# First attention layer of a four-layer network: both score maps in the array's rows, float32 values, rotation sums on VectorE

## The chip, the cores and the metric

The kernel runs on one core of one Trainium2 chip, in one launch. The metric is device time in microseconds (us). A core has TensorE (PE in the profile, with its weight loads as PEld), VectorE (DVE), ScalarE (ACT), GpSimd (POOL) and the queue that issues most DMAs (SP). Each engine works through its own instructions in the order in which they stand; semaphores tie the engines together. TensorE's results land in PSUM, from where DVE or ACT fetch them; POOL works on SBUF alone.

## The reference, cut to what matters

Two blocks of two layers each, 512 tokens, width 1024, all in float32. The change touches the attention of the first two layers:

```python
# layer 1: differential attention, 8 heads, two maps of 64 columns each, values of 128 columns
q = apply_rope(q, cos, sin) * 64 ** -0.5          # x1*cos - x2*sin, x1*sin + x2*cos
k = apply_rope(k, cos, sin)
for i in range(4):                                # blocks of 128 queries, keys up to the block's end
    sc = einsum('bqhmd,bkhmd->bhmqk', q[:, q0:kend], k[:, :kend])
    allowed = chunk(key) <= chunk(query)          # chunks of 64 tokens
    p = softmax(where(allowed, sc, neg))
    a = p[:, :, 0] - lam * p[:, :, 1]
    outs.append(einsum('bhqk,bkhe->bqhe', a, v[:, :kend]))
o = rms_norm(concat(outs), subln_g) * (1 - lambda_init)
x = layer_norm(alpha * x + o @ w_o);  x = layer_norm(alpha * x + swiglu(x))
# layer 2: attention over the own chunk and eight chunks before, 16 heads of 64, with a bias by distance
```

Then follow the second layer's feed-forward part and a second block of two layers (gated recurrences, a convolution and a feed-forward part), which the change leaves alone.

## The kernel before

Activations lie with features on the partitions and tokens along the row. A factor of a large product is held as two parts in the faster format fp32r: `hi`, a rounded copy that ACT writes (L150), and `lo`, the rest, which a subtraction on DVE writes (L151; POOL where `sub` is given). A product is three matmuls, hi·hi, hi·lo and lo·hi (`mm3`, L117 to L119; `dense`, L128 to L132). Plain float32 operands make one matmul in the code, which stands in the trace as two records.

**First layer (`attention_a`), about 25 to 306 us of the span.** For a head, `project` makes q, k (two maps each) and v from `xh`, `xl` and the weights `wA`, in four tiles of 128 tokens with 24 matmuls each. For each tile DVE forms four products with cos and sin out of PSUM (L379 to L382), POOL makes a difference and a sum of them (L383, L384), and v is split in hi and lo. `turn` transposes the rotated tiles and splits them (`qh`, `ql`, `kh`, `kl`). For a query block i of n = 128(i+1) keys, `scores` runs for each of the two maps a product of 64 rows, and a matmul of one row that adds the mask to the last 64 keys (L410); then DVE takes the maximum (L412) and ACT the exponential with its sum (L414). A map has a PSUM tile `sc` of its own, of which there are two. `mix` scales and subtracts the maps (L421 to L424), transposes the result (L427) and splits each of the 10 blocks of a head in `aTh` and `aTl`. `values` multiplies with v (`av`), forms the norm with matmuls of one column (L174), a chain of small DVE operations and matmuls against the identity (L202), and writes `oh`, `ol`.

`attend` takes head h block by block, and between blocks a tile of the projection of head h+1. Heads 0 to 5 go through all four blocks; heads 6 and 7 first through blocks 0 and 1, then 2 and 3, so that the first half of the output projection (`oh`, `ol` with `wo_a`, L128 to L132) has work for TensorE at the end. The framework's scheduler sorts all instructions by priority and its own estimate of time; `tc.high_priority` lets a group go ahead.

**Second layer (`attention_b`), about 720 to 942 us.** It already has the pattern that the change brings to the first: one tile `scs` of two banks for two heads, whose matmuls of 64 rows alternate (L541), a DVE instruction that adds the bias and takes the extreme in one pass (L546), the exponential in place (L548), transposes (L555), one copy for a whole block row from `tr` to `aT` on ACT (L558) and float32 value products (L566).

Of the kernel before, what the change touches and what calls it, by code (L numbers as in the profile page):

```python
# [18 lines left out]
P = 128  # L19
# [25 lines left out]
AT_OFF = (0, 512, 896, 1152, 1280)  # L45
HID1 = ((0, 5), (5, 10), (10, 14), (14, 22))
# [281 lines left out]
def attention_a(c):  # L328
    nc, tc, ap = c.nc, c.tc, c.ap
    with ExitStack() as st:  # L330
# [18 lines left out]
        nc.vector.tensor_scalar_sub(nlam[:, 1:2], nlam[:, 1:2], lambda_init(0))  # L349
        gsub = one.tile([P, 1], F32, name="gsub")  # L350
# [9 lines left out]
        def project(h):  # L360
            w = c.weight(ap["wA"][h], KT, 384, 2, then=load_x if h == 0 else None)
            v = [c.t(pool, [P, 4, P], F32R, t) for t in ("vh", "vl")]
            rots = c.t(pool, [P, 4, 4, 64], F32, "rot", 2)
            if h == 0:
                pss = [c.t(psum, [P, SEQ], F32, t, n) for t, n in (("sc", 2), ("sc", 2), ("av", 1))] + [c.bank()]
                c.dense_tk([ps[:, :384] for ps in pss], w, [(tt * P, tt * P + P) for tt in range(4)])
            for tt in range(4):
# [5 lines left out]
                qk = ps[:, :256].rearrange("p (g x) -> p g x", g=4)  # L373
                cs = cos[:, tt:tt + 1, :].to_broadcast([P, 4, 32])
                sn = sin[:, tt:tt + 1, :].to_broadcast([P, 4, 32])
                rot = rots[:, tt]
                tmp = c.t(pool, [P, 4, 64], F32, "rtmp")
                x1, x2 = qk[:, :, 0:32], qk[:, :, 32:64]
# [22 lines left out]
        def scores(h, i):  # L401
            qh, ql, kh, kl = made[h][0]
            n = (i + 1) * P
            qs = slice(i * P, i * P + P)
            ps_, sums = [], c.t(pool, [P, 2], F32, "sums")
            for m in range(2):
                ms = slice(m * 64, m * 64 + 64)
                sc = c.t(psum, [P, 512], F32, "sc", 2)
                c.mm3(sc[:, :n], qh[ms, qs], ql[ms, qs], kh[ms, :n], kl[ms, :n], True, False)
                nc.tensor.matmul(sc[:, n - 64:n], c.maskl, c.maskr, start=False, stop=True)  # L410
                mx = c.t(pool, [P, 1], F32, "mx")
                nc.vector.tensor_reduce(mx, sc[:, :n], AX.X, ALU.max, negate=True)  # L412
                p = c.t(pool, [P, SEQ], F32, f"p{m}", 3)
                nc.scalar.activation(p[:, :n], sc[:, :n], AF.Exp, bias=mx, scale=1.0, accum_out=sums[:, m:m + 1])  # L414
                ps_.append(p)
            return ps_, sums

        def mix(i, ps_, sums, aT):
# [9 lines left out]
            for j in range(i + 1):  # L428
                f = AT_OFF[j] + (i - j) * P
                c.split(*(t[:, f:f + P] for t in aT), tr[:, j * P:j * P + P])  # L430

        def values(h, aT, r0, r1):
# [3 lines left out]
            for j in range(r1):  # L436
                f = max(r0 - j, 0) * P
                t = slice(AT_OFF[j] + f, AT_OFF[j] + (r1 - j) * P)
                c.mm3(o[:, j * P + f:b], v[0][:, j, :], v[1][:, j, :], aT[0][:, t], aT[1][:, t], j == 0, j == r1 - 1)
# [12 lines left out]
        def attend(h, r0, r1, fill, last):  # L452
# [3 lines left out]
            aT = [c.t(pool, [P, 1280], F32R, t, 1) for t in ("aTh", "aTl")]  # L456
# [1043 lines left out]
```

## Time and profile before

| | us |
|---|---|
| median of 3 runs | 2801.31 |
| lowest, highest | 2797.56, 2808.92 |
| the profiled execution | 2814.44 |
| its span | 2812.4 |
| PE, PEld busy in the span | 2681.8 (95%), 2462.6 (88%) |
| DVE, ACT, POOL busy | 1955.0 (70%), 1228.4 (44%), 868.9 (31%) |

The profiled execution is 13 us longer than the median of the others. Ends of matmuls are modelled, so the time that a matmul takes up is read from its start to the start of the next one, not from its length. The granted clock (PEclk) is 1.00 at TensorE's full 2.4 GHz, 0.50 at 1.2 GHz. In a timeline, "x2" merges neighbours of one kind, and a bracket gives the idle time ahead of an instruction and who ended it.

### The profile page before, as it was taken

Reading aid. Unit: us, or ns where it says so; the run is one execution under the profiler, and the core shown is the slowest. Engines: PE = TensorE matmul, PEld = TensorE weight load, DVE = VectorE, ACT = ScalarE, POOL = GpSimd, SP = SyncE. Lnnn points to the kernel's source line nnn. Section 1 sums busy time; section 2 is a strip of 40 time slices with the busy share of each in tenths; the row PEclk is TensorE's granted clock in tenths of the full one; section 3 lists DMA queues with packets and bytes.
Section 4 is the critical chain, followed back from the end, with each engine's and each line's share of the span. In section 5 each row is a group of like instructions: output and inputs, shape, how many; then the busy total and the mean of one; then the engine's idle time right before and its main releaser. Section 6 shows DMA issues by size and latency. Waiting matters only on the chain. (4 is left out here: it accounts for less than half of the span.)

```text
span 2812.4 us, 49226 instructions
## 1 busy us (share of the span) xinstructions
PE 2681.8 (95%) x19432; PEld 2462.6 (88%) x19432; DVE 1955.0 (70%) x3974; ACT 1228.4 (44%) x2325; POOL 868.9 (31%) x711
## 2 busy tenths in 40 slices
PE   8999899999999999999999998999899999899997
PEld 7888899999777899899788898999898889889997
DVE  6775777676534777677766468888955645888895
ACT  4343444444544554444533335444533333445452
POOL 1110225572230225463012006545401200454550
PEclk9997999999999999999999999999999999999998
DMA  4111223323322222323211221322321211223222
GB/s 131 46 48 61 73 78 106 91 91 105 106 77 89 82 89 91 96 93 102 64 61 46 61 87 35 98 97 100 96 78 54 60 53 53 60 95 100 95 79 70
DMA packets 73799, 224.69 MB, mean 80 GB/s; under 512 B 9248, under 2 KB 11344, under 8 KB 73568
## 3 DMA queue, kind: packets, MB, share of 16 engines
q1 hardware_dynamic: 70736, 217.22, 24.8%
q8 instruction: 152, 2.49, 0.4%
q10 hardware_dynamic: 2304, 3.15, 0.3%
q0 software_dynamic: 528, 1.19, 0.1%
q14 instruction: 79, 0.65, 0.1%
HBM read 219.43 MB, written 2.10 MB: 79 GB/s over the span
## 5 line engine op out<-in xcount | busy, mean ns | idle before, releaser
L128 PE MATMUL mm<-xh,whi 128*128 128x256 f32 (+4 forms) x1976 | 583.9, 296 | 23.2 <-ACT tail L1254 11.3
L130 PE MATMUL mm<-xl,whi 128*128 128x256 f32 (+4 forms) x1976 | 580.4, 294 | 0.6 <-DVE xl L151 0.6
L132 PE MATMUL mm<-xh,wlo 128*128 128x256 f32 (+4 forms) x1976 | 578.6, 293 | 0.0
L151 DVE TENSOR_TENSOR wlo<-wraw,whi 128x1024 fp32r<-128x1024 f32 (+3 forms) x426 | 474.7, 1117 | 100.0 <-ACT whi L150 98.8
L150 ACT CAST whi<-wraw 128x1024 fp32r<-128x1024 f32 (+3 forms) x444 | 384.8, 883 | 326.3 <-PE mm L130 150.2
L128 PEld LDWEIGHTS mm<-xh,whi 128*128 128x128 f32 x1976 | 376.5, 191 | 39.7 <-ACT tail L1254 11.7
L130 PEld LDWEIGHTS mm<-xl,whi 128*128 128x128 f32 x1976 | 376.5, 191 | 8.3 <-issue 2.4
L132 PEld LDWEIGHTS mm<-xh,wlo 128*128 128x128 f32 x1976 | 377.5, 191 | 5.6 <-issue 1.3
L655 POOL TENSOR_TENSOR rawu<-rawu 128x512 f32<-128x512 f32 x76 | 120.6, 1587 | 547.5 <-DMA rawu<-in_wup 275.9
L151 DVE TENSOR_TENSOR wlo<-rawu,whi 128x1024 fp32r<-128x1024 f32 x152 | 204.7, 1347 | 110.4 <-ACT whi L150 110.3
L150 ACT CAST whi<-rawu 128x1024 fp32r<-128x1024 f32 x152 | 159.3, 1048 | 211.9 <-POOL rawu L658 172.1
L128 PE MATMUL u<-xh,whi 128*128 128x256 f32 (+2 forms) x680 | 193.6, 285 | 3.5 <-ACT gu L687 3.5
L128 PE MATMUL st<-hh,whi 128*128 128x256 f32 (+2 forms) x672 | 181.8, 324 | 15.0 <-ACT hh L150 7.5
L130 PE MATMUL u<-xl,whi 128*128 128x256 f32 (+2 forms) x680 | 193.1, 284 | 0.0
L132 PE MATMUL u<-xh,wlo 128*128 128x256 f32 (+2 forms) x680 | 193.1, 284 | 0.0
L130 PE MATMUL st<-hl,whi 128*128 128x256 f32 (+2 forms) x672 | 178.0, 319 | 4.3 <-DVE hl L151 4.3
L132 PE MATMUL st<-hh,wlo 128*128 128x256 f32 (+2 forms) x672 | 177.2, 318 | 0.0
L117 PE MATMUL mm<-whi,xh 128*128 128x384 f32 (+4 forms) x520 | 173.3, 333 | 0.0
L118 PE MATMUL mm<-wlo,xh 128*128 128x384 f32 (+4 forms) x520 | 171.4, 330 | 0.0
L119 PE MATMUL mm<-whi,xl 128*128 128x384 f32 (+4 forms) x520 | 171.0, 329 | 0.0
L128 PE MATMUL mm<-hh,whi 128*128 128x256 f32 (+1 forms) x512 | 147.0, 289 | 12.7 <-ACT hh L150 12.7
L658 POOL TENSOR_TENSOR rawu<-rawu 128x512 f32<-128x512 f32 x76 | 111.4, 1466 | 120.1 <-DVE wlo L151 120.1
(426 smaller groups left out, 7077.3 us busy)
## 6 DMA issues: line engine op xcount, KB each, us to landing
wraw<-in_wup SPq DMA_DIRECT2D x100, 512.0 KB, 4.3
rawu<-in_wup SPq DMA_DIRECT2D x76, 512.0 KB, 3.6
wraw<-in_wdn SPq DMA_DIRECT2D x64, 320.0 KB, 3.6
wraw<-in_w_in SPq DMA_DIRECT2D x40, 512.0 KB, 3.6
wraw<-in_wdn SPq DMA_DIRECT2D x32, 512.0 KB, 4.4
wraw<-in_wA SPq DMA_DIRECT2D x32, 384.0 KB, 3.3
wraw<-in_wdn SPq DMA_DIRECT2D x32, 256.0 KB, 3.3
wraw<-in_wqk_b SPq DMA_DIRECT2D x16, 512.0 KB, 3.7
```

What stands on the lines that cost most here:

```text
L117: mm(out, sh, mh, start=start, stop=False)
L118: mm(out, sh, ml, start=False, stop=False)
L119: mm(out, sl, mh, start=False, stop=stop)
L128: mm(o, wh, xh[k], start=first, stop=False)
L130: mm(o, wh, xl[k], start=False, stop=False)
L132: mm(o, wl, xh[k], start=False, stop=last)
L150: nc.scalar.copy(hi, src)
L151: (sub or nc.vector.tensor_sub)(lo, src, fp(hi))
L655: sub(T3, B22, B12)
L658: sub(B22, B22, B12)
```

## The change

In the first layer:
- `scores` runs both maps into one PSUM tile of two banks (`sc`, of which there is one now): hi·hi for map 0 and map 1, then hi·lo, then lo·hi, ahead of other work by `high_priority`. Map 0 sits in rows 0 to 63 of the array, map 1 in rows 64 to 127. The mask matmul goes; a mask in SBUF is added in the DVE pass that takes the extreme (as L546 does), and the exponential works in place from SBUF.
- v and the transposed probabilities stay in float32: one ACT copy of v for each tile, one ACT copy for a block row in place of up to four pairs of a cast and a subtraction, and one matmul in place of three. `aT` has two buffers.
- The rotation is two DVE products of 256 columns and two DVE sums; POOL leaves it.
- For heads 1 to 7 the `lo` parts of `wA` are subtracted on POOL.

In the second layer the copy from `tr` to `aT` goes from ACT to DVE.

```diff
@@ project
-            w = c.weight(ap["wA"][h], KT, 384, 2, then=load_x if h == 0 else None)
-            v = [c.t(pool, [P, 4, P], F32R, t) for t in ("vh", "vl")]
+            w = c.weight(ap["wA"][h], KT, 384, 2, then=load_x if h == 0 else None,
+                         sub=nc.gpsimd.tensor_sub if h > 0 else None)
+            v = c.t(pool, [P, 4, P], F32, "v")
...
-                nc.vector.tensor_mul(rot[:, :, 0:32], x1, cs)
-                nc.vector.tensor_mul(rot[:, :, 32:64], x1, sn)
-                nc.vector.tensor_mul(tmp[:, :, 0:32], x2, sn)
-                nc.vector.tensor_mul(tmp[:, :, 32:64], x2, cs)
-                nc.gpsimd.tensor_sub(rot[:, :, 0:32], rot[:, :, 0:32], tmp[:, :, 0:32])
-                nc.gpsimd.tensor_add(rot[:, :, 32:64], rot[:, :, 32:64], tmp[:, :, 32:64])
-                c.split(v[0][:, tt, :], v[1][:, tt, :], ps[:, 256:384])
+                nc.vector.tensor_mul(rot, qk, cos[:, tt:tt + 1, :].to_broadcast([P, 8, 32]))
+                nc.vector.tensor_mul(tmp, qk, sin[:, tt:tt + 1, :].to_broadcast([P, 8, 32]))
+                nc.vector.tensor_sub(rot[:, 0:8:2], rot[:, 0:8:2], tmp[:, 1:8:2])
+                nc.vector.tensor_add(rot[:, 1:8:2], rot[:, 1:8:2], tmp[:, 0:8:2])
+                nc.scalar.copy(v[:, tt, :], ps[:, 256:384])
@@ scores
+            with tc.high_priority(offset=2000):
+                sc = c.t(psum, [P, 2, SEQ], F32, "sc", 1)
+                for k, (u, w) in enumerate(((qh, kh), (qh, kl), (ql, kh))):
+                    for m in range(2):
+                        ms = slice(m * 64, m * 64 + 64)
+                        nc.tensor.matmul(sc[:, m, :n], u[ms, qs], w[ms, :n], start=k == 0, stop=k == 2)
             for m in range(2):
-                ms = slice(m * 64, m * 64 + 64)
-                sc = c.t(psum, [P, 512], F32, "sc", 2)
-                c.mm3(sc[:, :n], qh[ms, qs], ql[ms, qs], kh[ms, :n], kl[ms, :n], True, False)
-                nc.tensor.matmul(sc[:, n - 64:n], c.maskl, c.maskr, start=False, stop=True)
-                mx = c.t(pool, [P, 1], F32, "mx")
-                nc.vector.tensor_reduce(mx, sc[:, :n], AX.X, ALU.max, negate=True)
                 p = c.t(pool, [P, SEQ], F32, f"p{m}", 3)
-                nc.scalar.activation(p[:, :n], sc[:, :n], AF.Exp, bias=mx, scale=1.0, accum_out=sums[:, m:m + 1])
+                nc.vector.tensor_tensor_reduce(p[:, :n], sc[:, m, :n], mask[:, SEQ - n:], -1.0, 3.0e38, ALU.add, ALU.min,
+                                               mx[:, m:m + 1])
+                nc.scalar.activation(p[:, :n], p[:, :n], AF.Exp, bias=mx[:, m:m + 1], scale=-1.0,
+                                     accum_out=sums[:, m:m + 1])
@@ mix, values
-            for j in range(i + 1):
-                f = AT_OFF[j] + (i - j) * P
-                c.split(*(t[:, f:f + P] for t in aT), tr[:, j * P:j * P + P])
+            nc.scalar.copy(aT[:, i:4 * i + 1:3, :], tr[:, :n].rearrange("p (j x) -> p j x", x=P))
...
-                c.mm3(o[:, j * P + f:b], v[0][:, j, :], v[1][:, j, :], aT[0][:, t], aT[1][:, t], j == 0, j == r1 - 1)
+                nc.tensor.matmul(o[:, i * P:b], v[:, j, :], aT[:, 3 * j + i:3 * j + r1, :], start=j == 0, stop=j == r1 - 1)
@@ attention_b, attend
-                    nc.scalar.copy(to, tr[:, :n].rearrange("p (j x) -> p j x", x=P))
+                    nc.vector.tensor_copy(to, tr[:, :n].rearrange("p (j x) -> p j x", x=P))
```

Three places show how the order moves. TensorE inside head 2, around the scores of its second query block, before (`mm` is the projection of the next head, `tr` a transposed probability block):

```order
L119 MATMUL mm_1086<-whi_1079,xl 128x384
L117 MATMUL sc_1123<-kh_987,qh_985 128x256
L118 MATMUL sc_1123<-kl_988,qh_985 128x256
L119 MATMUL sc_1123<-kh_987,ql_986 128x256
L410 MATMUL sc_1123<-maskr,maskl 128x64
L117 MATMUL sc_1132<-kh_987,qh_985 128x256
L118 MATMUL sc_1132<-kl_988,qh_985 128x256
L119 MATMUL sc_1132<-kh_987,ql_986 128x256
L410 MATMUL sc_1132<-maskr,maskl 128x64
L427 MATMUL tr_1146<-ident,p_175_1011 128x128
```

The same place now:

```order
L120 MATMUL mm_953<-whi_935,xl 128x384
L415 MATMUL sc_987<-kh_867,qh_865 128x256 x2
L415 MATMUL sc_987<-kl_868,qh_865 128x256 x2
L415 MATMUL sc_987<-kh_867,ql_866 128x256 x2
L118 MATMUL mm_953<-whi_935,xh 128x384
L119 MATMUL mm_953<-wlo_936,xh 128x384
L120 MATMUL mm_953<-whi_935,xl 128x384
L118 MATMUL mm_953<-whi_941,xh 128x384
L119 MATMUL mm_953<-wlo_942,xh 128x384
```

The mask products are gone, the two maps alternate, and the next query block's scores (into the same buffer) stand eight projection matmuls further down, seven before the one after that, where 24 stood each time before.

DVE at the end of a head, around the rotation of the last tile, before (`aTl` and `wlo` are subtractions, `ql` belongs to the next head's scores):

```order
L424 SCALAR_TENSOR_TENSOR p_156_907<-p_156_907,rr_967,p_159_916 128x512
L379 TENSOR_TENSOR rot_727<-mm_933,cosA 128x4x32
L380 TENSOR_TENSOR rot_727<-mm_933,sinA 128x4x32
L381 TENSOR_TENSOR rtmp_958<-mm_933,sinA 128x4x32
L382 TENSOR_TENSOR rtmp_958<-mm_933,cosA 128x4x32
L151 TENSOR_TENSOR aTl_763<-tr_972,aTh_762 128x128
L151 TENSOR_TENSOR wlo_1080<-wraw_1077,whi_1079 128x768
L151 TENSOR_TENSOR vl_726<-mm_933,vh_725 128x128
```

And now:

```order
L383 TENSOR_TENSOR rot_648<-mm_823,cosA 128x256
L384 TENSOR_TENSOR rtmp_848<-mm_823,sinA 128x256
L385 TENSOR_TENSOR rot_648<-rot_648,rtmp_848 128x4x32
L386 TENSOR_TENSOR rot_648<-rot_648,rtmp_848 128x4x32
L155 SCALAR_TENSOR_TENSOR ql_866<-tr_869,qh_865 128x512
L152 TENSOR_TENSOR kl_868<-tr_876,kh_867 128x512
```

The sums of the rotation (L385, L386) stand on DVE behind their products, and the subtractions for weights, v and probabilities have left this queue.

TensorE at the end of the layer, from the scores of head 6's last block on, before (head 7's next scores follow; `mm` from `oh` and `ol` is the output projection):

```order
L119 MATMUL sc_2878<-kh_2419,ql_2418 128x512
L410 MATMUL sc_2878<-maskr,maskl 128x64
L130 MATMUL mm_3142<-ol_99,whi_3096 128x256
L132 MATMUL mm_3142<-oh_98,wlo_3097 128x256
L130 MATMUL mm_3168<-ol_99,whi_3102 128x256
L132 MATMUL mm_3168<-oh_98,wlo_3103 128x256
L132 MATMUL mm_3195<-oh_98,wlo_3109 128x256
L128 MATMUL mm_3195<-oh_98,whi_3108 128x256
L174 MATMUL av_2848<-ones_h,sq_2844 128x1 x2
L130 MATMUL mm_3195<-ol_99,whi_3108 128x256
```

And now:

```order
L415 MATMUL sc_2474<-kh_2083,ql_2082 128x512 x2
L445 MATMUL av_2446<-aT_2392,v_2167 128x256
L445 MATMUL av_2446<-aT_2392,v_2167 128x128
L133 MATMUL mm_2746<-oh_89,wlo_2660 128x256
L415 MATMUL sc_2516<-kh_2336,qh_2334 128x384 x2
L415 MATMUL sc_2516<-kl_2337,qh_2334 128x384 x2
L415 MATMUL sc_2516<-kh_2336,ql_2335 128x384 x2
L175 MATMUL av_2453<-ones_h,sq_2449 128x1 x2
L435 MATMUL tr_2492<-ident,p_487_2440 128x128 x3
L415 MATMUL sc_2559<-kh_2336,qh_2334 128x512 x2
```

The output projection that stood between the last scores now stands before them: from here to the values of head 6 a single matmul of it is left.

## Rows read from the trace of the kernel before

**Rows 1.** Busy time by stretch: us, PE, PEld, DVE, ACT, POOL; PEclk, DMA, GB/s

```profile
25.00:247.00 222.00, 219.97 (x1201) 191.35 (x1199) 160.15 (x512) 90.72 (x257) 29.58 (x64) 0.95 0.20 57
247.00:285.00 38.00, 38.00 (x127) 29.32 (x128) 16.74 (x65) 9.28 (x31) 0.00 (x0) 0.51 0.08 26
285.00:306.00 21.00, 18.65 (x141) 17.05 (x140) 15.29 (x60) 7.62 (x20) 1.89 (x2) 0.98 0.00 1
...
720.00:942.00 222.00, 215.39 (x1387) 168.42 (x1386) 95.97 (x314) 111.76 (x279) 46.39 (x24) 1.00 0.28 85
...
65.00:70.00 5.00, 5.00 (x21) 4.42 (x21) 2.01 (x9) 1.46 (x6) 0.87 (x2) 0.53 0.00 0
```

**Rows 2.** Timeline of TensorE (start, us, what): first scores of heads 4, 5, 6

```profile
156.91 0.33 PE L117 MATMUL sc<-kh,qh 64*128 64x128 f32 x2
...
187.72 0.33 PE L117 MATMUL sc<-kh,qh 64*128 64x128 f32 x2
...
221.31 0.33 PE L117 MATMUL sc<-kh,qh 64*128 64x128 f32 x2
```

**Rows 3.** TensorE, first layer: scores of 512 keys, then most of those of 128

```profile
144.62 0.50 PE L117 MATMUL sc<-kh,qh 64*128 64x512 f32 x1
...
145.51 0.29 PE L410 MATMUL sc<-maskr,maskl 1*128 1x64 f32 x1
...
146.84 0.55 PE L427 MATMUL tr<-ident,p 128*128 128x128 f32 x3
...
158.28 0.32 PE L118 MATMUL sc<-kl,qh 64*128 64x128 f32 x1
...
159.45 1.05 PE L174 MATMUL av<-ones_h,sq 128*128 128x1 f32 x8
```

**Rows 4.** TensorE, second layer: scores of two heads, 512 keys, then 128

```profile
893.68 0.51 PE L541 MATMUL sc<-kh,qh 64*128 64x512 f32 x2
...
894.58 0.50 PE L128 MATMUL mm<-xh,whi 128*128 128x512 f32 x1
...
897.18 0.33 PE L541 MATMUL sc<-kh,qh 64*128 64x128 f32 x2
...
897.84 0.63 PE L555 MATMUL tr<-ident,p 128*128 128x128 f32 x4
```

**Rows 5.** TensorE, first layer: an fp32r value product, and four float32 products

```profile
133.70 1.05 PE L202 MATMUL av<-ident,ry 128*128 128x128 f32 x8
134.51 0.42 PE L118 MATMUL mm<-wlo,xh 128*128 128x384 f32 x1
...
153.73 0.39 PE L119 MATMUL av<-aTh,vl 128*128 128x512 f32 x1
153.95 0.34 PE L117 MATMUL av<-aTh,vh 128*128 128x384 f32 x1
```

**Rows 6.** Groups by form (count, busy us, mean ns, idle before): DVE, DVE, POOL, POOL

```profile
L546 DVE CUSTOM_DVE_ANT_0 p<-sc,bias 128x512 f32<-128x512 f32 x16 | 10.5, 683 | 1.3 <-PE sc L541 1.3
...
L424 DVE SCALAR_TENSOR_TENSOR p<-p,rr,p 128x512 f32<-128x512 f32 x8 | 5.9, 742 | 0.0
...
L384 POOL TENSOR_TENSOR rot<-rot,rtmp 128x128 f32<-128x128 f32 x32 | 16.4, 512 | 0.0
...
L151 POOL TENSOR_TENSOR wlo<-wraw,whi 128x1024 fp32r<-128x1024 f32 x18 | 42.9, 2394 | 109.7 <-ACT whi L150 109.7
```

**Rows 7.** Timeline: a DVE subtraction and a POOL sum at one time

```profile
28.84 1.24 DVE L151 TENSOR_TENSOR wlo<-wraw,whi 128x768 fp32r<-128x768 f32 x1
...
29.22 1.18 POOL L384 TENSOR_TENSOR rot<-rot,rtmp 128x128 f32<-128x128 f32 x1
```

**Rows 8.** Waits of TensorE's weight loads, second layer: total us, times, longest

```profile
PEld sc L541 <- DVE mx L546: 4.8, 12, 0.6
PEld av L566 <- ACT aT L558: 4.5, 16, 0.5
```

**Rows 9.** Timeline of TensorE: its wait before the low clock at the layer's end

```profile
245.42 0.44 PE L397 MATMUL tr<-ident,rot 128*128 128x128 f32 x2 [1.55 <-POOL rot L384]
```

More of the change, by code (lines that the diff above doesn't have):

```diff
@@ L45 @@
 AT_OFF = (0, 512, 896, 1152, 1280)
+AT_BLOCKS = 13
 HID1 = ((0, 5), (5, 10), (10, 14), (14, 22))
@@ L349, in attention_a @@
         nc.vector.tensor_scalar_sub(nlam[:, 1:2], nlam[:, 1:2], lambda_init(0))
+        mask = one.tile([P, SEQ], F32, name="mask")
+        nc.gpsimd.memset(mask, 0.0)
+        nc.gpsimd.memset(mask[0:64, SEQ - 64:], NEG)
         gsub = one.tile([P, 1], F32, name="gsub")
@@ L360, in project @@
         def project(h):
-            w = c.weight(ap["wA"][h], KT, 384, 2, then=load_x if h == 0 else None)
-            v = [c.t(pool, [P, 4, P], F32R, t) for t in ("vh", "vl")]
+            w = c.weight(ap["wA"][h], KT, 384, 2, then=load_x if h == 0 else None,
+                         sub=nc.gpsimd.tensor_sub if h > 0 else None)
+            v = c.t(pool, [P, 4, P], F32, "v")
             rots = c.t(pool, [P, 4, 4, 64], F32, "rot", 2)
             if h == 0:
-                pss = [c.t(psum, [P, SEQ], F32, t, n) for t, n in (("sc", 2), ("sc", 2), ("av", 1))] + [c.bank()]
+                two = c.t(psum, [P, 2, SEQ], F32, "sc", 1)
+                pss = [two[:, 0], two[:, 1], c.t(psum, [P, SEQ], F32, "av", 1), c.bank()]
                 c.dense_tk([ps[:, :384] for ps in pss], w, [(tt * P, tt * P + P) for tt in range(4)])
@@ L372, in project @@
                     c.dense_t(ps[:, :384], w, tt * P, tt * P + P)
[L373 to L378, printed above, removed]
[L379 to L385 removed]
+                qk = ps[:, :256].rearrange("p (g x) -> p g x", x=32)
+                rot = rots[:, tt].rearrange("p g (h x) -> p (g h) x", h=2)
+                tmp = c.t(pool, [P, 8, 32], F32, "rtmp")
+                nc.vector.tensor_mul(rot, qk, cos[:, tt:tt + 1, :].to_broadcast([P, 8, 32]))
[3 more added lines that the diff above has]
+                nc.scalar.copy(v[:, tt, :], ps[:, 256:384])
                 if tt == 3:
@@ L436, in values @@
             for j in range(r1):
[L437 to L439 removed]
+                i = max(r0, j)
+                nc.tensor.matmul(o[:, i * P:b], v[:, j, :], aT[:, 3 * j + i:3 * j + r1, :], start=j == 0, stop=j == r1 - 1)
             sq = c.t(pool, [P, SEQ], F32, "sq", 1)
@@ L455, in attend @@
             next(fill, None)
-            aT = [c.t(pool, [P, 1280], F32R, t, 1) for t in ("aTh", "aTl")]
+            aT = c.t(pool, [P, AT_BLOCKS, P], F32, "aT", 2)
             for i in range(r0, r1):
@@ L1316, in constants @@
     nc.vector.memset(c.ones_h, 1.0 / P)
-    ml = cp.tile([1, P], F32, name="maskl0")
-    nc.vector.memset(ml, 0.0)
-    nc.vector.memset(ml[:, 0:64], 1.0)
-    mr = cp.tile([1, 64], F32, name="maskr0")
-    nc.vector.memset(mr, NEG)
-    c.maskl = cp.tile([1, P], F32R, name="maskl")
-    nc.vector.tensor_copy(c.maskl, ml)
-    c.maskr = cp.tile([1, 64], F32R, name="maskr")
-    nc.vector.tensor_copy(c.maskr, mr)
     c.ln_g = load("ln_g", [P, 4, KT])
```

1 line of the change is left out of this document (added).

## The prediction

> **What bounds the kernel now.** I read the busy time by stretch first, because the change sits in one stage. From 25 to 247 us TensorE is busy 219.97 of 222 us, VectorE 160, ScalarE 91 and GpSimd 30 [rows 1]. So in heads 0 to 6 TensorE has no gaps to give back: what takes time is the number and kind of its matmuls, and the clock that it gets. Everything that the change takes from VectorE and ScalarE is worth nothing there unless a wait of TensorE's ends with it. Heads are counted by the start of their first scores: head 4 lasts 187.72 − 156.91 = 30.81 us, head 5 221.31 − 187.72 = 33.59 [rows 2].
>
> Second, the clock. The mean over 25 to 247 us is 0.95: some 222 × 0.05 / 0.5 = 22 us at half clock, in short spells, one of which is at 65 to 70 us, where TensorE is busy 5.00 of 5 us at 0.53 [rows 1]. Head 5's 2.8 us over head 4 are my price for a spell. From 247 to 285 us TensorE is busy all the time at 0.51: 19 us of work at full clock takes 38 [rows 1]. Ahead of this stretch stands a wait of 1.55 us for the rotation's sum on GpSimd [rows 9]. From 285 us on the clock is back and TensorE idles 2.35 of 21 us [rows 1].
>
> Third, the second layer, because it already has the pattern: pairs of 64 rows, a bias added in the pass that takes the extreme, float32 values. It runs 222 us with TensorE busy 215 at clock 1.00 [rows 1], so this pattern as such doesn't cost the clock there.
>
> **The scores.** A block of 512 keys takes 2.22 us from its first matmul to the next work (144.62 to 146.84); the mask matmul starts 0.89 in, so of 1.11 for a map the mask is about 0.22 [rows 3]. The pattern to come takes 0.90 in the second layer (893.68 to 894.58) [rows 4]: 1.32 saved. With 128 keys, from the record at 158.28 to the next work at 159.45 it is 1.17 [rows 3], and the hi·hi pair ahead of that record starts earlier; with about 0.25 for that pair I estimate 1.42 against at most 0.66 [rows 4]: 0.76 saved. The blocks of 256 and 384 keys lie between; the mean of the ends, 1.04, times four blocks is 4.2 us for a head, with ends 3.0 and 5.3.
>
> **The values.** A head has 1280 columns of them. Before, three fp32r products of 0.22 for 512 columns [rows 5]: 3 × 1280/512 × 0.22 = 1.65 us. After, one float32 product, of which four with 128 columns take 0.81 (133.70 to 134.51) [rows 5]: 1280/512 × 0.81 = 2.03. So +0.4 for a head; ends 0 (if one wide matmul costs a fifth less than four narrow ones) and +1.3 (if all blocks together cost 45% more for a column than these four).
>
> **New waits for the one `sc` buffer.** Both maps now share it, so scores of the next block start only when VectorE's two passes over the last have ended. Two refills in a head come eight and seven projection matmuls later, the third right behind other short work; before, 24 matmuls stood between. The second layer has the same hand-over: 4.8 us of TensorE's waiting in 12 waits, the longest 0.6 [rows 8], and its pass takes 683 ns at 512 keys [rows 6]. Spread over its 32 refills that is 0.15 each, so for three refills 0.45 to 1.8 us for a head. I take 1.0: behind the waiting score stands the whole of TensorE's queue, since it works in order, and VectorE's own queue in a head is longer than in the second layer (160 against 96 of 222 us [rows 1]).
>
> **Rotation and weights.** The rotation's two sums go from GpSimd (512 ns each [rows 6]) to VectorE behind its products, which helps the last tile, whose transposes TensorE waits for, as at 245.42 [rows 9]. In exchange GpSimd gets the `lo` weights: 2394 ns for 1024 columns [rows 6], an estimated 1.8 for 768, four times a head, 7.2 of some 30 us. In the trace a VectorE subtraction with both inputs in SBUF at 28.84 took 1.24 and a GpSimd sum begun inside it 1.18, over twice its mean of 512 ns [rows 6, 7]: where both run, one holds up the other. The new sums on VectorE are of that kind. Two of them stand ahead of the head's last transposes; each meets a weight subtraction with a chance of 7.2/30 and then loses half of 1.8: 2 × 0.24 × 0.9 = 0.4, of which the shorter hand-over gives a little back. I take 0.3 for a head, ends 0 and 1.8. The Trainium skill, "SBUF — State Buffer", section "Who interferes with whom", says that a VectorE instruction with two SBUF inputs and a GpSimd instruction that reads SBUF share a read port, and that the one which comes first keeps it to its end. The 1.18 above agrees; taken for every one of the last sums the rule gives 1.8 a head where I take 0.3, and this is the second rival below.
>
> At the layer's start head 1's `lo` weights now take 1.8 on GpSimd where VectorE needed 1.24 [rows 7]; TensorE can be waiting there. −1 us, ends 0 and −3.
>
> **What I cost at nothing.** VectorE loses the subtractions of weights, v and probabilities; ScalarE gets one copy for several casts; neither bounds these heads [rows 1]. The scaling pass of 742 ns (L424) [rows 6] stays. If VectorE's relief reaches TensorE at all it is in the `sc` waits, where it is counted. In the second layer the copies move from ScalarE (112 of 222 us) to VectorE (96) [rows 1]. They end 16 waits with 4.5 us together [rows 8]; on VectorE they queue ahead of the passes that end the other 4.8 [rows 8]. The one can gain what the other loses: 0, ends ±3.
>
> **The layer's end.** After 245 us there remain two blocks of head 6 and four of head 7: by the above 1.1 + 1.3 + 4.2 = 6.6 us less score work at full clock. Most of it lies in the half-clock stretch, where a microsecond of work counts two: up to 13, and I take 12. Against that, the output projection that stood between the last scores now stands ahead of them. So TensorE waits for VectorE's passes and sums there: the last four blocks need four pairs of passes and four scaling pairs, each up to 0.68 and 0.74 [rows 6], against a few microseconds of matmuls left. That wait is between 1.5 and 10 us; I take 3, since head 7's early blocks are short. Together +9, ends 2 and 16.
>
> **The sum.** A head: 4.2 − 0.4 − 1.0 − 0.3 = 2.5 us. Six heads give 15, head 6's first two blocks 1, the start −1, the end 9, the second layer 0: 24 us. The profiled execution is 2814.44 us, 13 above the median, so it would go to about 2790; nothing in the sum depends on those 13 us, so I take the same 24 off the median: 2801 − 24 = **2777**. Its own range: ±1.3 for a head (the terms' ends combined, not added), so ±8 for six, and ±7 for the end, together about ±11: 2766 to 2788.
>
> **Rivals.**
> 1. The clock comes back. With less queued, the spells in the heads may vanish (three spells at 2.8 us, 8) and part of the half-clock stretch at the layer's end with them (38 us hold 19 of lost time; a third of it is 6 to 7): 15 more, 2762. For it: the second layer's pattern runs at 1.00 [rows 1], and the wait of 1.55 ahead of the long stretch is for a sum that leaves GpSimd [rows 9]. Against: at 65 to 70 us the clock is low while TensorE is fully busy [rows 1], so fewer waits need not change it.
> 2. VectorE and GpSimd hold each other up on every head's last sums: 1.5 more a head, 9, and 3 at the start: a gain of 12, 2789. For it, the 1.18 [rows 7]; against, GpSimd is free for three quarters of a head, and its subtractions come when weights land, not when tiles end.
> 3. The pairs don't run side by side, so the change doesn't do what it says. Then a head saves only the mask, 8 × 0.22 = 1.8, less 0.4, 1.0 and 0.3: about nothing, 2800. Against: 0.90 against 2.22 in the second layer with the same shapes [rows 3, 4].
> 4. The other side: the three new waits for `sc` break up TensorE's stream, and the clock falls in mid-head and stays. Time at half clock costs half of itself, so the 24 us are gone once it grows by 48 us. If heads 4 and 5 ran at half clock throughout, their 64 us [rows 2] would nearly double: +62, 2839. For it: the long low stretch follows a wait of 1.55 [rows 9]. Against: the second layer has the same refill waits [rows 8] and keeps 1.00 [rows 1].
>
> **How the numbers follow.** Forecast 0.60, rival 1 0.17, rival 2 0.13, rival 3 0.04, rival 4 0.06. The range goes from below rival 1's time to rival 3's, 2754 to 2800; outside lie rival 4 and the far ends of the first two, under 0.2. Half a per cent is 14 us, about what a measurement of this kernel can tell from no change. Faster by more than that, under 2787: nearly all of the forecast's own range (0.53), rival 1 (0.17), a third of rival 2 (0.04): 0.74. Slower: rival 4 and a little, 0.07. The rest, 0.19, is the same.
>
> **What would show it.** First-layer score blocks near 0.9 us at 512 keys and 0.66 at 128; undisturbed heads of about 28.3 us; waits of `sc` for VectorE's passes, about 1 us a head; the second layer's stretch still 222 us. Rival 1 would show in the granted clock of heads and of the layer's end, rival 2 in rotation sums on VectorE that take 1 to 2 us beside GpSimd's subtractions. What would make me wrong most easily is the end of the layer, whose term is a third of the sum and rests on waits that the trace of before doesn't show.

## The result and the profile after

The changed kernel takes 2780.18 us (median of four runs, 2775.7 to 2783.3) against 2805.11 (four runs, 2797.56 to 2818.66): a ratio of 0.9898, 95% interval 0.9866 to 0.9931. The gain is 25 us where 24 was forecast. Its profiled execution has a span of 2775.1 us.

Two stretches can be laid beside each other: the heads, from head 0's first scores to head 7's, and the end, from there to the first matmul of the feed-forward part. The lines give us, PE, PEld, DVE, ACT, POOL; PEclk, DMA, GB/s. The change, with the second layer's stretch that answers to 720 to 942 of before:

```profile
33.19:235.18 201.99, 190.34 (x1099) 161.65 (x1098) 128.53 (x432) 86.80 (x213) 39.92 (x22) 0.96 0.21 58
235.18:309.40 74.22, 66.72 (x496) 60.30 (x496) 55.22 (x180) 30.78 (x71) 13.83 (x14) 0.98 0.23 68
685.10:907.10 222.00, 218.14 (x1412) 171.53 (x1411) 120.96 (x376) 89.57 (x214) 45.77 (x24) 1.00 0.28 85
```

The same heads and end in the trace of before that the prediction read:

```profile
32.04:246.91 214.87, 213.32 (x1160) 185.51 (x1159) 154.19 (x491) 87.76 (x250) 25.38 (x56) 0.95 0.19 55
246.91:342.80 95.89, 91.30 (x536) 80.12 (x536) 59.66 (x187) 33.01 (x83) 13.82 (x14) 0.79 0.18 56
```

In a second trace of the kernel before (e4 below), then in a second trace of the change (e10):

```profile
32.12:238.09 205.97, 204.43 (x1161) 177.91 (x1161) 154.36 (x491) 87.85 (x250) 25.40 (x56) 1.00 0.19 56
238.09:324.20 86.11, 81.52 (x536) 72.72 (x536) 59.55 (x187) 32.90 (x83) 13.81 (x14) 0.90 0.20 63
```

```profile
34.19:233.98 199.79, 188.23 (x1100) 161.85 (x1099) 128.25 (x431) 86.71 (x213) 39.93 (x22) 0.97 0.20 59
233.98:307.90 73.92, 66.80 (x496) 60.45 (x496) 55.27 (x180) 30.83 (x71) 13.84 (x14) 0.98 0.23 69
```

A stretch times one minus its clock is the time lost to the clock, and the rest is what the stretch takes at full clock. The clock is printed to two places, so an entry is good to about 1 us for the heads and 0.5 for the end:

| us | heads, full clock | lost | end, full clock | lost |
|---|---|---|---|---|
| before, two traces | 204.1, 206.0 | 10.7, 0 | 75.8, 77.5 | 20.1, 8.6 |
| change, two traces | 193.9, 193.8 | 8.1, 6.0 | 72.7, 72.4 | 1.5, 1.5 |
| difference of the means | -11.2 | +1.7 | -4.1 | -12.9 |

Read in narrower windows the heads' differences are -12.1 and +2.6, with the same sum. Head 0 starts 1.6 us later in the mean, and what follows the two stretches takes 2469.6 and 2469.9 us before, 2465.7 and 2471.9 with the change: -1. Together -26, which is the medians' difference. So in these four traces half of the gain is clock at the layer's end. The spans and mean clocks of all timed runs say the same of the whole program: the four runs of the change lose 39 to 47 us to the clock, 44 in the mean, 33 runs of the kernel before, made beside the experiments, 39 to 73, 58 in the mean; without that the change takes 2733 us and the kernel before 2748, 15 less.

TensorE, which had no gaps in heads 1 to 5 before, now idles about 2 us in each of heads 0 to 4. This is the end of head 4 on TensorE (answers to [rows 2] and [rows 9]):

```profile
172.87 0.55 PE L399 MATMUL tr<-ident,rot 128*128 128x128 f32 x3
175.27 0.69 PE L399 MATMUL tr<-ident,rot 128*128 128x128 f32 x2 [1.85 <-DVE rot L386]
175.75 3.13 PE L445 MATMUL av<-aT,v 128*128 128x512 f32 x4
178.81 0.33 PE L415 MATMUL sc<-kh,qh 64*128 64x128 f32 x2
```

The last two transposes wait 1.85 us for a sum of the rotation, and behind them two value products (four records) take 3.1 us, nearly twice their time, at half clock (head 0's take 1.67). VectorE there, then GpSimd (answers to [rows 7]):

```profile
171.79 0.42 DVE L383 TENSOR_TENSOR rot<-mm,cosA 128x256 f32<-128x256 f32 x1 [3.22 <-PE mm L120]
172.14 0.41 DVE L384 TENSOR_TENSOR rtmp<-mm,sinA 128x256 f32<-128x256 f32 x1
172.59 0.82 DVE L385 TENSOR_TENSOR rot<-rot,rtmp 128x128 f32<-128x128 f32 x1
173.33 1.88 DVE L386 TENSOR_TENSOR rot<-rot,rtmp 128x128 f32<-128x128 f32 x1
```

```profile
169.62 5.44 POOL L152 TENSOR_TENSOR wlo<-wraw,whi 128x768 fp32r<-128x768 f32 x3 [23.23 <-ACT whi L151]
...
173.22 1.84 POOL L152 TENSOR_TENSOR wlo<-wraw,whi 128x768 fp32r<-128x768 f32 x1
```

Three weight subtractions run back to back from 169.62 to 175.06. Both sums begin inside one and end about 0.15 us behind it: 0.82 and 1.88 us for an instruction that takes 0.28 elsewhere. Each subtraction follows a cast on ScalarE, and the casts start as matmuls of the projection's last tile let go of the buffers:

```profile
169.75 0.84 ACT L151 CAST whi<-wraw 128x768 fp32r<-128x768 f32 x1 [0.20 <-PE mm L120]
```

Two more answers. The scores of 512 keys take 157.52 - 156.63 = 0.89 us ([rows 3]: 2.22):

```profile
156.63 0.50 PE L415 MATMUL sc<-kh,qh 64*128 64x512 f32 x2
156.96 0.40 PE L415 MATMUL sc<-kl,qh 64*128 64x512 f32 x2
...
157.52 1.16 PE L203 MATMUL av<-ident,ry 128*128 128x128 f32 x8
```

And of the groups of the first layer by form (count, busy us, mean ns, idle before; answers to [rows 6]), VectorE's pass over 512 keys is as long as in the second layer before, and GpSimd's subtraction as estimated:

```profile
L152 POOL TENSOR_TENSOR wlo<-wraw,whi 128x768 fp32r<-128x768 f32 x25 | 45.4, 1836 | 135.3 <-ACT whi L151 133.8 <-PE tr L399 1.4 <-DVE rtmp L384 0.2
...
L419 DVE CUSTOM_DVE_ANT_0 p<-sc,mask 128x512 f32<-128x512 f32 x16 | 10.4, 685 | 0.0
```

The second layer, from its first scores to the first matmul of its feed-forward part, before and with the change (columns as above), all at full clock:

```profile
723.16:985.94 262.78, 254.10 (x1701) 206.40 (x1701) 127.17 (x399) 128.13 (x310) 57.88 (x37) 1.00 0.29 89
688.23:947.10 258.87, 253.88 (x1701) 206.53 (x1701) 153.52 (x463) 107.93 (x245) 56.76 (x37) 1.00 0.30 88
```

The same matmuls take 3.9 us less: TensorE idles 5.0 us in place of 8.7. The second traces, e4 and e10, give 262.79 and 258.94.

### The profile page after: what moved, and what is told of

Read it like the earlier page. It is cut to its first block, busy times and chain, and to the rows that moved or that the text cites. A ratio compares the mean times of both kernels' runs of the same rounds, so it can differ in the third digit from the quotient of the medians.

```text
span 2775.1 us, 48832 instructions
## 1 busy us (share of the span) xinstructions
PE 2636.2 (95%) x19332; PEld 2421.5 (87%) x19332; DVE 1949.3 (70%) x3957; ACT 1204.8 (43%) x2213; POOL 890.2 (32%) x677
## 5 line engine op out<-in xcount | busy, mean ns | idle before, releaser
L152 DVE TENSOR_TENSOR wlo<-wraw,whi 128x1024 fp32r<-128x1024 f32 (+3 forms) x398 | 447.8, 1128 | 90.0 <-ACT whi L151 88.7
L661 POOL TENSOR_TENSOR rawu<-rawu 128x512 f32<-128x512 f32 x76 | 119.6, 1574 | 549.5 <-DVE ry L192 150.9
L152 DVE TENSOR_TENSOR wlo<-rawu,whi 128x1024 fp32r<-128x1024 f32 x152 | 204.1, 1342 | 116.4 <-ACT whi L151 116.2
L152 POOL TENSOR_TENSOR wlo<-wraw,whi 128x768 fp32r<-128x768 f32 (+1 forms) x46 | 94.2, 2063 | 257.6 <-ACT whi L151 252.9
```

Of the source, the lines that this page charges most:

```text
L152: (sub or nc.vector.tensor_sub)(lo, src, fp(hi))
L661: sub(T3, B22, B12)
```

## The experiments

"Head" is the time of an undisturbed head at full clock, read between first scores as in [rows 2].

| kernel | median us | ratio to before, 95% | head, us |
|---|---|---|---|
| before | 2805 to 2809 | 1 | 30.8 |
| the change | 2780.2 | 0.9866 to 0.9931 | 29.2 |
| e1 weights on VectorE | 2762.6 | 0.9805 to 0.9886 | 27.2 to 27.5 |
| e2 rotation, weights as before | 2769.0 | 0.9826 to 0.9892 | 27.4 |
| e3 scores alone | 2769.3 | 0.9829 to 0.9896 | 27.4 |
| e5 weights in halves | 2771.7 | 0.9861 to 0.9902 | 28.7 |
| e6 product in PSUM | 2777.6 | 0.9871 to 0.9921 | 28.3 |
| e7 e1 with old values | 2767.7 | 0.9844 to 0.9885 | 27.3 |
| e8 e1 with copies on ScalarE | 2765.8 | 0.9835 to 0.9876 | 27.3 |
| e9 mask alone | 2770.9 | 0.9857 to 0.9903 | 27.6 |
| e11 e1 with a delay | 2763.5 | 0.9826 to 0.9870 | 27.4 |
| e12 masks behind both maps | 2808.4 | 0.9975 to 1.0023 | 29.9 |

**The wait at the heads' ends: e1, e2.** The change without GpSimd's share of the weights:

```diff
             w = c.weight(ap["wA"][h], KT, 384, 2, then=load_x if h == 0 else None,
-                         sub=nc.gpsimd.tensor_sub if h > 0 else None)
+                         )
```

> The changed kernel with one part undone: the lo parts of the first layer's weights are subtracted on VectorE again, the rotation's sums stay there. Theory A (GpSimd's weight subtraction holds up the rotation's last sum, and the wait of 1.9 us that TensorE gets from it at the end of heads 0 to 4 also costs the half-clock spell behind it): the last sum takes 0.3 instead of 1.88 us, the five waits go (5 x 1.9 = 9.5) and with them the spells of heads 1 to 4 (4 x 1.8 = 7): about 2763 us against 2780. Rival B (the wait goes, the spells have another cause): about 2770. Rival C (VectorE's four extra subtractions of about 1 us a head stand ahead of the rotation and put the wait back): 2780 or more, with TensorE's transposes still waiting for the rotation.

The waits are gone, and the time is theory A's, 2762.6. That the number fits is partly luck. In the trace the heads give 18.9 us: 12 at full clock, where the forecast had 9.5 for the waits, and 7 of clock in them, as forecast. But over all four runs e1 loses as much to the clock as the change does, 47 us against 44 in the mean. So the gain that all runs show, 18 us, is time at full clock. In the timeline of VectorE the last sums are short again:

```profile
131.97 0.29 DVE L384 TENSOR_TENSOR rot<-rot,rtmp 128x128 f32<-128x128 f32 x1
132.19 0.28 DVE L385 TENSOR_TENSOR rot<-rot,rtmp 128x128 f32<-128x128 f32 x1
```

What TensorE itself waited for in the heads (us, times, longest) has no rotation left; in the change the first line of that list was 9.2 us in 5 waits for it:

```profile
PE av L175 <- DVE os L448: 0.9, 5, 0.2
PE sc L414 <- ACT kh L151: 0.3, 1, 0.3
```

The order moved too: some value products now stand ahead of the last transposes, so not all of the gain need be the hold-up's (e5 keeps the order). This kernel has the lowest median of all (e11 can't be told from it), and is faster than the kernel before and the change. The intervals of e1 and the change meet between 0.9866 and 0.9886, but the slowest of e1's four runs (2769.39) is 6 us below the fastest of the change's (2775.7).

e2 takes back the rotation as well (four products on VectorE, sums on GpSimd, as in the deleted lines of the change):

> The changed kernel with the rotation as it was (four products on VectorE, sums on GpSimd) and the weights' lo parts on VectorE: scores, values and second-layer copies stay new. Theory A: no instruction of 1.8 us stands in the way of the sums, so the waits of 1.9 at the heads' ends go; GpSimd's sums are slower (0.5 each), so about 2767. If the clock at the layer's end (38 us at 0.51 before, 0.97 now) came back because the sums left GpSimd, the long half-clock stretch returns here and the time is about 2780 or more; if it came back because of the scores or values, it stays.

2769, and the end keeps its clock (one spell, at 235 to 245 us). So the clock there did not come from the sums leaving GpSimd. Whether the rotation on VectorE is worth anything over the old one (e1 against e2) lies within the intervals.

**Size of the hold-up: e5, e6.** e5 halves GpSimd's instruction.

```diff
+        def half_sub(lo, src, hi):
+            for a in (0, 384):
+                nc.gpsimd.tensor_sub(lo[:, a:a + 384], src[:, a:a + 384], hi[:, a:a + 384])
...
-                         sub=nc.gpsimd.tensor_sub if h > 0 else None)
+                         sub=half_sub if h > 0 else None)
```

> The changed kernel, but GpSimd subtracts the weights' lo parts in two halves of 384 columns; everything on TensorE and VectorE stands in the same order. Theory A (VectorE's sum waits for the whole GpSimd instruction that began before it): the longest wait falls from 1.85 to about 0.9 us, the last sum from 1.88 to about 1.0, TensorE's wait at the ends of heads 0 to 4 from 1.85 to some 0.9; 5 us less, and up to 7 more if the shorter wait no longer costs the clock: 2768 to 2776 against 2780 of the change and 2763 without the overlap. Rival (the two share bandwidth and both just run slower): halves change nothing, 2780.

TensorE's and VectorE's order is the change's, so only the length differs. The time, 2771.7, lies in theory A's range. The sums end with the running half, 1.10 and 1.08 us, and TensorE's wait falls from 1.85 to 1.32:

```profile
108.92 1.10 DVE L389 TENSOR_TENSOR rot<-rot,rtmp 128x128 f32<-128x128 f32 x1
109.94 1.08 DVE L390 TENSOR_TENSOR rot<-rot,rtmp 128x128 f32<-128x128 f32 x1
```

A shared bandwidth would not follow the length of the other's instruction; this does. The wait did not halve, because each of the two sums meets a half of its own. In e6 the second product overwrites the projection in PSUM:

```diff
-                tmp = c.t(pool, [P, 8, 32], F32, "rtmp")
+                tmp = qk
```

> The changed kernel, but the rotation's second product stays in PSUM (written over the projection), so that each of the two sums on VectorE reads one operand from SBUF and one from PSUM; GpSimd still subtracts the weights. Theory A in the form that only two operands from SBUF collide with GpSimd: the sums take about 0.3 us beside a running GpSimd subtraction, the waits of 1.85 go and the spells with them, about 2763 or a little less, since VectorE has 4 us less to do in a head than without GpSimd's help. Rival (any VectorE instruction that touches SBUF is held up by GpSimd's): the sums still take up to 1.9, about 2780.

Half of this came true. With one operand in PSUM all 29 sums of each line take 275 to 289 ns (min/median/max below), also those that run inside a GpSimd subtraction:

```profile
L385 DVE TENSOR_TENSOR rot<-rot,mm x29: 275/288/289, 30.3 to 229.2; 128x128 f32<-128x128 f32 x29
L386 DVE TENSOR_TENSOR rot<-rot,mm x29: 275/280/284, 30.5 to 229.4; 128x128 f32<-128x128 f32 x29
```

The time did not follow: the scores now wait for ScalarE's cast of kh, 6.7 us in 6 waits up to 1.3, where e1 had 0.3. In this trace ScalarE's copy of v waits for the sums to be done with the bank, and the heads lose 12 us to half-clock spells; at full clock they take 188 us against 194 of the change. What sends the cast late was not tried further.

```profile
PE sc L415 <- ACT kh L151: 6.7, 6, 1.3
```

The Trainium skill ("SBUF — State Buffer", section "Who interferes with whom") has this as a rule: two SBUF operands on VectorE and a reading GpSimd instruction exclude each other for the whole of the one that came first. The change, e5 and e6 agree with it in size (1.88, 1.08 and 0.28 us) and in its condition.

**Which part saves: e3, e9, e12.** e3 puts the change's `scores` (with its mask tile) alone into the kernel before.

> The kernel before with the new scores alone (both maps in the array's rows, the mask added on VectorE, one sc buffer ahead of other work, exponential in place); values, rotation, weights and second-layer copies as before. The prediction's terms: 4.2 us a head less 1.0 of waits for sc, so 3.2 x 6 + 2 for the heads and up to 9 at the end: 2775 to 2783 against 2805. If the layer's end gets its clock back from the scores, about 10 less at the end. Rival: the scores save nothing on the path and the gain came from the values: 2800.

2769.3, heads of 27.4, within 0.2 us of e1's: more than was forecast for this part, and below the whole change. e9 moves only the mask and keeps the two maps one after the other in two tiles:

```diff
-                c.mm3(sc[:, :n], qh[ms, qs], ql[ms, qs], kh[ms, :n], kl[ms, :n], True, False)
-                nc.tensor.matmul(sc[:, n - 64:n], c.maskl, c.maskr, start=False, stop=True)
+                c.mm3(sc[:, :n], qh[ms, qs], ql[ms, qs], kh[ms, :n], kl[ms, :n], True, True)
-                nc.vector.tensor_reduce(mx, sc[:, :n], AX.X, ALU.max, negate=True)
...
+                nc.vector.tensor_tensor_reduce(p[:, :n], sc[:, :n], mask[:, SEQ - n:], -1.0, 3.0e38, ALU.add, ALU.min, mx)
```

> The kernel before with the mask alone moved: no mask matmul, the mask added on VectorE in the pass that takes the extreme, exponential from SBUF; the two maps still one after the other in two PSUM tiles, all else as before. The prediction's split of a head's score saving: 8 x 0.22 = 1.8 us for the mask, the remaining 2.4 for the pairs side by side. So an undisturbed head of 30.8 - 1.8 = 29.0 us and about 2793 against 2807 (e3, with the pairs too, has heads of 27.35 and 2769). Rival (the mask matmul of one row costs more than its place in the queue, for instance by the layer's end at half clock): 2785 or less, and the low stretch at the layer's end gone.

The expectation failed: not 1.8 but 3.2 us a head, 2770.9 us, as much as e3; the time is the rival's (2785 or less). Its timeline of TensorE shows why:

```profile
128.14 0.51 PE L117 MATMUL sc<-kh,qh 64*128 64x512 f32 x2
128.48 0.40 PE L118 MATMUL sc<-kl,qh 64*128 64x512 f32 x2
128.72 0.40 PE L119 MATMUL sc<-kh,ql 64*128 64x512 f32 x2
129.04 0.55 PE L429 MATMUL tr<-ident,p 128*128 128x128 f32 x3
```

In the program as built, TensorE's queue has map 0's three matmuls of this block ahead of map 1's three. They run in twos all the same, 0.90 us for the block as in the alternating order. e9 also shows whose the clock is: with nothing but the mask moved, its four runs lose 42 to 50 us to the clock, 45 in the mean, against 56 of the seven runs of the kernel before beside them. e12 then keeps the mask matmuls and moves them behind both maps:

```diff
+            with tc.high_priority(offset=2000):
+                for k, (u, w) in enumerate(((qh, kh), (qh, kl), (ql, kh))):
+                    for m in range(2):
+                        ms = slice(m * 64, m * 64 + 64)
+                        nc.tensor.matmul(scs[m][:, :n], u[ms, qs], w[ms, :n], start=k == 0, stop=False)
+                for m in range(2):
+                    nc.tensor.matmul(scs[m][:, n - 64:n], c.maskl, c.maskr, start=False, stop=True)
```

> The kernel before with the two mask matmuls of a block moved behind the scores of both maps (two PSUM tiles as before, ahead of other work by priority as in the change); they are still computed. e9 saved 3.2 us a head by leaving the mask matmuls out, with the two maps one after the other in the program, and its trace shows them side by side all the same. Theory D (the mask matmul of map 0, which uses rows of the array that map 0 uses, stood between the maps and kept map 1 from starting): the maps overlap here too, a block of 512 keys takes 0.90 + 2 x 0.22 = 1.34 us against 2.22, a head about 29.4 against 30.8 and 27.6, the time about 2788. Rival E (the mask matmuls cost their own time and no more, and the overlap in e9 comes from something else): blocks of about 2.2 us, heads of 30.8, about 2805.

The time is that of the kernel before. But the scheduler gave a comparison within one trace: in the blocks of 128 to 384 keys both masks stand behind both maps, in the blocks of 512 of heads 1 to 5 map 0's mask stands between them. First a block of 256 keys, then one of 512:

```profile
161.52 0.39 PE L411 MATMUL sc<-kh,qh 64*128 64x256 f32 x2
...
162.08 0.40 PE L413 MATMUL sc<-maskr,maskl 1*128 1x64 f32 x2
162.41 0.44 PE L119 MATMUL mm<-whi,xl 128*128 128x384 f32 x1
```

```profile
136.92 0.49 PE L411 MATMUL sc<-kh,qh 64*128 64x512 f32 x1
...
137.81 0.29 PE L413 MATMUL sc<-maskr,maskl 1*128 1x64 f32 x1
138.03 0.49 PE L411 MATMUL sc<-kh,qh 64*128 64x512 f32 x1
...
138.93 0.29 PE L413 MATMUL sc<-maskr,maskl 1*128 1x64 f32 x1
139.15 0.45 PE L117 MATMUL mm<-whi,xh 128*128 128x384 f32 x1
```

The scores of 256 keys go in twos (0.56 us) and the two masks add 0.33. The 512 block takes 2.23 us in ones, as before the change. The same block of 256 keys in the kernel before, with the mask between, takes 163.65 - 162.12 = 1.53 us against 0.89 here:

```profile
162.12 0.38 PE L117 MATMUL sc<-kh,qh 64*128 64x256 f32 x1
...
163.65 0.33 PE L427 MATMUL tr<-ident,p 128*128 128x128 f32 x1
```

So theory D holds where the masks stand behind, and the one-row matmul between the maps is what kept them apart; why it does (the rows that it shares with map 0, or something else) no run shows. The rest of the expectation failed: the undisturbed head is 29.9, not 29.4, since the blocks of 512 saved nothing, and in this trace five heads have half-clock spells that cost 22 us together. The ten runs say that the saving was there and the clock took it: without the time lost to it they take 2737 us against 2748 of the twelve runs of the kernel before beside them, and they lose 70 us in the mean against 59.

**The other parts: e7, e8.** e7 gives e1 the old values (the deleted lines of `project`, `mix` and `values` are back).

> As e1_weights_on_dve, and the values as before the change too (v and the transposed probabilities in hi and lo, three matmuls for one, a cast and a subtraction for each block). The prediction charged 0.4 us a head to the new values on TensorE (3 us for 8 heads) and nothing for the work that VectorE loses: then about 2760 here against 2763 of e1. Rival (the subtractions on VectorE that the new values save do reach TensorE, through the waits for scores or at the layer's end): 2766 or more.

2767.7 against 2762.6, with intervals that overlap and heads alike to 0.1 us. By its number this is the rival's case, but e1's four runs reach from 2760.5 to 2769.4, and without the time lost to the clock both take 2715 to 2716 us in the mean. Neither the forecast charge of 0.4 a head nor a gain shows. e8 is one word:

```diff
-                    nc.vector.tensor_copy(to, tr[:, :n].rearrange("p (j x) -> p j x", x=P))
+                    nc.scalar.copy(to, tr[:, :n].rearrange("p (j x) -> p j x", x=P))
```

> As e1_weights_on_dve, and the second layer's copies of probabilities on ScalarE again. The prediction put this part at 0, ends 3 either way: 2760 to 2766 against 2763 of e1, and the stretch from the first to the last scores of the second layer (206.5 us before, 207.0 after) shorter by at most 1 us. Rival: the copies on VectorE hide a gain or a loss of more than 3.

2765.8, in the forecast's range, and no difference that the medians can tell. The traces can. From the first scores to the first matmul of the last block's scores it is 206.5 us, against 207.0 in e1; but read on to the feed-forward part, e1 takes 3.9 us less than e8:

```profile
670.40:929.29 258.89, 253.93 (x1701) 206.55 (x1702) 153.56 (x463) 107.93 (x245) 56.76 (x37) 1.00 0.29 88
668.17:931.02 262.85, 254.13 (x1701) 206.43 (x1701) 127.27 (x399) 128.05 (x310) 57.90 (x37) 1.00 0.28 89
```

All traces with these copies on ScalarE have 262.8 to 263.1 us here, all with them on VectorE 258.3 to 259.3. So the copies on VectorE are worth about 3.9 us: the rival, which put more than 3 in them, was right.

**The clock: e4, e10, e11.** e4 is the kernel before unchanged.

> The kernel before, unchanged, for a second trace of it: whether the stretch of 38 us at half clock at the end of the first layer, and the three short spells in heads 1, 2 and 5, are there again. The changed kernel's trace is 37 us shorter than the first trace of before, the medians differ by 25. If the low stretches move from run to run, the second trace has them elsewhere or shorter and is some 10 us nearer to the median.

The spells move: none in the heads, and 8.6 instead of 20.1 us lost at the end. The span is 2794.1, 18 us shorter, and by the mean clocks of the two spans (0.984 and 0.978) nearly all of that is clock. e10 is the change unchanged.

> The changed kernel unchanged, for a second trace: if the half-clock spells at the ends of heads 1 to 4 follow from the waits of 1.85 us, they stand in the same places again; if they come and go as in the kernel before (three spells in its heads in one trace, none in the other), they are elsewhere. The waits themselves and the sums of 1.88 us stand there in either case.

The waits stand where they stood (TensorE's own waits: us, times, longest), but behind only two of the five is there a spell now, those of heads 3 and 4. Heads 1 and 2 have none and take 29.2 us, which is e1's 27.3 and the wait of 1.9:

```profile
PE tr L399 <- DVE rot L386: 9.2, 5, 1.9
```

e11 delays e1's last sums by five more products.

```diff
+                for _ in range(5 if tt == 3 and 0 < h < 6 else 0):
+                    nc.vector.tensor_mul(tmp, qk, sin[:, tt:tt + 1, :].to_broadcast([P, 8, 32]))
                 nc.vector.tensor_sub(rot[:, 0:8:2], rot[:, 0:8:2], tmp[:, 1:8:2])
```

> As e1_weights_on_dve, with five more rotation products (0.35 us apart) between the products and the sums of the last tile, for heads 1 to 5's projections: a delay of some 1.75 us that VectorE makes by itself, with GpSimd idle. If a late rotation costs by its lateness alone, waits of 1 to 1.8 us come back at the ends of heads 0 to 4 and the time goes to 2768 to 2772, with half-clock spells to about 2780. If the value products, which stand ahead of the last transposes here, cover the delay, it stays near 2763 to 2766, which shows what an order with that cover is worth.

2763.5: in this order all the value products stand ahead of the last transposes, and no wait for the rotation is left. So late sums cost nothing once something stands in front. That the change paid because the scheduler's estimate did not hold the hold-up, as it holds this delay, fits but is not shown. Since no wait came back, e11 does not say what a wait by itself does to the clock.

That stays open. Waits of 1.85 us are followed by a spell in six of ten cases (four in the first trace, two in the second), waits of 1.32 in e5 by none in those five heads, and e12 has four spells with no wait above 0.3 us ahead of them, and one behind a wait of 1.06. At the layer's end a wait of 2.1 us is followed by half clock within 2 us in all six traces that have it (the change's two, e2, e6, e8, e11). No run changed the clock alone.

## Why the prediction was right, and where it was not

The forecast of 2777, in a range of 2754 to 2800, met 2780.2. Its sum was 24 and the medians differ by 25. That they agree so closely is luck: two terms were off by some 7 us each in opposite directions, and two of the rivals, the first at the layer's end and the second in the heads, came true together and cancelled.

- **The bound, and the saving of a score block**: right. TensorE had no gaps in the heads, and the matmuls that went are what the heads gained. Blocks take 0.89 us at 512 keys and 0.25 + 0.37 = 0.62 at 128 (forecast 0.90 and at most 0.66). Read from start to start, the scores of an undisturbed head take 2.8 us in e3 and 7.1 before: 4.3 less, forecast 4.2. The third rival, maps that don't run side by side, did not come.
- **Whose saving it is**: the step that gave the mask 0.22 us a map and the rest to the alternating pairs was wrong. Leaving the mask matmuls out brings 3.2 us a head by itself (e9), since the maps then overlap in any order. The sum is the same, so the forecast did not feel it.
- **Waits for `sc`**: forecast 1.0 us a head, next to none in the heads. TensorE's own waits there name VectorE's pass not once, and its weight loads, from which the forecast was read ([rows 8]), 2.1 us in seven heads:

```profile
PEld sc L415 <- DVE mx L419: 2.1, 8, 0.4
```

  A head still gains 3.5 us in e3, not 4.3: the values and their norm take 0.5 more from start to start, the projection 0.3 (18.4 against 18.0). So the net fitted, its reason did not. At the layer's end, where little stands between the scores, the waits are there:

```profile
246.66 0.44 PE L415 MATMUL sc<-kh,qh 64*128 64x384 f32 x2 [0.92 <-DVE mx L419]
248.93 0.50 PE L415 MATMUL sc<-kh,qh 64*128 64x512 f32 x2 [0.57 <-DVE mx L419]
...
252.98 0.52 PE L435 MATMUL tr<-ident,p 128*128 128x128 f32 x3 [2.12 <-DVE rt L190]
```

- **The rotation's sums beside GpSimd**: the failed step. It took the meeting of a sum and a subtraction as chance, 7.2 of 30 us, and so 0.3 us a head. It is no chance: the last tile's matmuls free the weight buffers and end the projection that the rotation reads, so the subtractions and the sums start from the same matmuls. The wait came at the ends of heads 0 to 4, 1.85 each (at 5 and 6 the subtractions were over, and the sums took 0.28). An undisturbed head is 29.2 us for it, where 28.3 was forecast. This is the second rival, which had 0.13; its size was right (1.8), and its place too.
- **The heads' sum**: forecast 16 (15 and 1), measured 11.2 at full clock less 1.7 of clock: 9.5. In e1, without the hold-up and in a somewhat other order, it is 24 at full clock (183.09 us at 0.99, 181.3 at full clock, against 205). The spells in the heads did not vanish, as the first rival had it, nor did the clock stay low there, as the fourth had it.
- **The layer's end**: forecast 9, measured 17. At full clock 4.1 of it: forecast 6.6 of matmuls less 3 of waits, and the waits are above. The other 13 are clock: 20.1 and 8.6 us lost before, 1.5 in both traces of the change. This is the part of the first rival that was forecast at 6 to 7 for the end. The prediction counted the matmuls saved in a half-clock stretch twice, as if the stretch stayed. Over whole runs, moving the mask alone brings the loss down as far as the whole change does (e9 and the change, 45 and 44 us in the mean); values, rotation and alternating pairs aren't needed for it. All kernels without mask matmuls lost 1.5 to 7 us here, but so did e12 (5), which has them; by what the moved mask returns the clock is not settled.
- **Second layer**: forecast 0, ends 3 either way, because what the copies gain the passes could lose. Measured a gain of 3.9 us, outside these ends (e8, and the stretches to the feed-forward part). Within the scores it is a small loss: the first matmul of the last block's scores comes 0.5 us later and the last 2.3; the gain lies behind. In the times it is hidden by the spread of the clock.
- **Start, values**: -1 and small, as forecast (-1.6; no difference shown).

The single trace of before was one with much half clock: 37 us above the change's trace, 18 above the other trace of before. The prediction's choice to carry the gain over to the median, not the span, was right; it priced the heads' terms at full clock, and so the spells of that one trace did not enter their sum. The term for the layer's end did rest on that trace: 12 us for work that is 6.6 at full clock.

## What to carry to other kernels

Ask of every step that is moved to GpSimd whether VectorE has an instruction with both operands in SBUF at the same moment, and whether one event starts both: then they meet head after head, and the one waits for the whole of the other. A matmul of one row between two products that lie in different rows of the array costs the overlap of these products as well as itself; look at its place before rewriting the order around it. Take a second trace of the kernel before, if there is one, before pricing anything by a stretch at half clock. Read a stage to the first work of the next one, not to its own last piece: the second layer's gain stands behind its last scores.

## What was not expected of the hardware

Two products of 64 rows each, in different rows of the array, ran side by side although three matmuls of the one stood ahead of the first of the other in the built program (e9: six matmuls of 512 columns in 0.90 us, against 2 x 0.89 when the mask stood between). So for such pairs it does not hold to the letter that an engine takes its instructions in the order in which they stand. And the same program lost about 10 us to the clock in its heads in one execution and none in another.
